# A hybrid attention and convolution layer on one core: one tile's split moved ahead of another step, and a store issued two steps earlier

## The chip, the cores and the metric

The kernel runs on one core of one Trainium2 chip. The metric is the time of one execution on the device in microseconds (us). The engines are TensorE (PE, matrix products, with its weight loads as PEld), VectorE (DVE), ScalarE (ACT), GpSimd (POOL) and SyncE (SP, which here only issues DMAs). ACT issues DMAs too, between its own operations and in the same order of instructions.

## The reference

One layer over 4096 tokens of width 1024, in float32:

```python
h = rmsnorm(x, norm_w)
proj = h @ w_in                      # u, g_b, g_c, z_conv, q, k, v, z_attn: 512 columns each
y_conv = short_gated_conv(u, g_b, g_c, conv_w, conv_b) * silu(z_conv)
q, k = rmsnorm(q per head), rmsnorm(k per head)
for window, dilation in ((128, 1), (512, 4), (2048, 16)):
    o_i, lse_i = dilated_window_attention(q, k, v, rel_bias, window, dilation)
o = sum over i of softmax(lse)_i * o_i
y = concat(y_conv, o * silu(z_attn))
out = x + y @ w_out
```

There are 8 heads of 64; each query attends to a band of keys on both sides, in blocks of 128 queries by 256 keys.

## The kernel before

Products that need more than half precision are made of two float16 parts, `hi` and `lo`, so that each product is three matmuls (hi·hi, hi·lo, lo·hi).

**Phase A** (up to about 690 us of the trace) goes over 32 tiles of 128 tokens (loop at L594). For a tile `t` it makes, on PE, four groups of 24 matmuls (`mm`, lines 410 to 412): q, k, v and z. Each group accumulates in one of eight PSUM banks. Tiles 0 and 1 are done ahead of the loop, side by side. The tile's input is its normalised `x`, transposed: `x_split(t)` copies `x` times its norm to float16 on ACT (L391, tile `xs`), takes the difference on DVE (L392), and issues two DMA transposes on SP (L394) that write the tile `hb`, which the matmuls of tile `t` read. Inside the loop, `x_split(t + 2)` stands at the end of tile `t`, so tile 4 is split in the loop's first turn, tile 2 in front of the loop, and tile 3 in the first turn (`t == 2`) by a line of its own, next to `late()`.

`late()` holds what is left to do for tiles 0 and 1: `v_sums` (eight matmuls of L484 into bank 3, read by DVE at L485), `v_scales` (L488, L489), `post_v` of tiles 0 and 1 (L457 to L461, with a store to `v_d`), `v_gate` (L493, L494), and `post_z` of tiles 0 and 1 (L465 on ACT, L466 on DVE, L467 on POOL, then a store to `sz_d` on SP). L485 frees bank 3 for tile 2's z group; L457 of tile 0 frees bank 4 for tile 3's q group. `post_qk1` (L424, L426) starts the work on a tile's q or k behind its matmuls; `post_z` ends a tile. In some turns a task for the convolution's weights stands behind `x_split`, with one sum on DVE (L275) that a small matmul on PE (L278) reads.

**Phase B** (about 690 to 1840 us) goes over 384 units `u` of attention (loop at L1162), 8 units to a group, 48 groups. While PE works through attention it fills its time with the matmuls of the convolution (`fill`, lines 854 to 856). In step `u` stand, in this order: `p_hi(u)` on ACT (L1098, or L1092 for each third unit), `p_lo(u)` on DVE, `exps(u + 1)` on ACT (L1066), a DMA transpose of the probabilities on SP (`tr`, L1112, tile `pt`; each third unit goes through PE instead, `tr_pe`, L1086, which reads `L`, the output of L1066), `av(u - 3)` on PE (L1123 to L1125) with its eviction on ACT (L1126) into `ot`, the products of `u + 2` (L1044, L1045) and its `logits` on DVE (L1057), which write into `ot` too. `ot` has two buffers, one per group; a group's outputs go to memory by `o_store` (L1137, L1139 or L1141, on ACT's queue), and the next group but one can only write the buffer when the store has read it. `b` is a unit's place in its group; since `av` runs three units late (`LAG = 3`), the last eviction of a group is in step `b == 2` of the next group. In step `b == 3`, `load_v` issues the loads of the next group's `vt`, three to eight DMAs on ACT's queue.

Every DMA of the program, on whichever queue, is given one of eight completion semaphores in turn (`DMAHW0` to `DMAHW7`), and one that gets a semaphore again waits on its issuing engine until the DMA eight places before it has landed. The order of the work is written by hand; each engine runs its instructions in that order.

Of the kernel before, what the change touches and what calls it, by code (L numbers as in the profile page):

```python
# [56 lines left out]
LAG = 3  # L57
# [8 lines left out]
def tile_hybrid_block(  # L66
# [135 lines left out]
    def load_x(t):  # L202
        XT[t] = xts[t % 3]
        nc.sync.dma_start(XT[t], xf[t * 128:(t + 1) * 128, :])
# [149 lines left out]
    def stats1(t):  # L354
        sq = pa.tile([128, D], F16, name="xsq")
        ss = pa.tile([128, 1], F32, name="ssx", bufs=2)
        nc.scalar.activation(sq, XT[t], AF.Square, accum_out=ss)
        RX[t] = rsqrt1(ss, 1, 1.0 / D, "x")
# [4 lines left out]
    def h_views(t):  # L363
        c = t // 2
        b = (hb[c] if t % 2 else h_room(c, c % 3))[:, t % 2]
        HT[t] = (b[:, 0], b[:, 1])
        return HT[t]
# [20 lines left out]
    def x_split(t):  # L388
        parts = [pa.tile([128, D], F16, name=f"xs{i}", bufs=2) for i in range(2)]
        r = RX.pop(t)  # L390
        nc.scalar.activation(parts[0], XT[t], AF.Copy, scale=r)  # L391
        nc.vector.scalar_tensor_tensor(parts[1], XT[t], r, parts[0], op0=OP.mult, op1=OP.subtract)  # L392
        for to, src in zip(h_views(t), parts):
            nc.sync.dma_start(to, src, transpose=True)  # L394
# [5 lines left out]
    def h_store(c):  # L400
        nc.sync.dma_start(hT_d[c], hb.pop(c).rearrange("p a b k n -> p (a b k n)"))
# [20 lines left out]
    def post_qk1(t, which, p):  # L422
        sq = pa.tile([128, 512], F32, name="wk", bufs=3)
        nc.scalar.activation(sq, p, AF.Square)  # L424
        ss = pa.tile([128, H], F32, name="ssq", bufs=2)
        nc.vector.tensor_reduce(ss, sq.rearrange("p (h d) -> p h d", h=H), axis=AX.X, op=OP.add)  # L426
        PQ[t, which] = (p, rsqrt1(ss, H, rqs[:, int(which == "k"), 0:1], "q"))

    def post_qk2(t, which):
        p, rs = PQ.pop((t, which))  # L430
        c = rqs[:, int(which == "k")]
        r = rsqrt2(rs, c[:, 1:2], c[:, 2:3])
        qn = pa.tile([128, H, DH], F32, name="wk", bufs=3)
        nc.vector.tensor_tensor(qn, p.rearrange("p (h d) -> p h d", h=H),
                                r[:, :, None].to_broadcast([128, H, DH]), op=OP.mult)
        if which == "q":
            nc.vector.tensor_tensor(qn, qn, cvec[:, None, :].to_broadcast([128, H, DH]), op=OP.mult)  # L437
        w, hi, lo = (4, slice(0, 4, 3), slice(1, 3)) if which == "q" else (6, slice(0, 4, 2), slice(4, 6))
        q16 = pa.tile([128, 4, w, DH], F16, name="h16", bufs=3)
        qn = qn.rearrange("p (a b) d -> p a b d", b=2)  # L440
        nc.scalar.activation(q16[:, :, hi], qn, AF.Copy)  # L441
        nc.vector.tensor_tensor(q16[:, :, lo], qn, q16[:, :, hi], op=OP.subtract)
        if which == "k":
            nc.gpsimd.tensor_copy(q16[:, :, 1:4:2], q16[:, :, hi])
        Q16[t, which] = q16
# [8 lines left out]
    def post_v(t, p):  # L454
        v16 = pa.tile([128, H, 128], F16, name="h16", bufs=3)
        v32 = pa.tile([128, 512], F32, name="wk", bufs=3)
        nc.vector.tensor_tensor(v32, p, vs, op=OP.mult)  # L457
        pv = v32.rearrange("p (h d) -> p h d", h=H)
        nc.scalar.activation(v16[:, :, 0:DH], pv, AF.Copy)
        nc.vector.tensor_tensor(v16[:, :, DH:128], pv, v16[:, :, 0:DH], op=OP.subtract)  # L460
        nc.sync.dma_start(v_d[t * 128:(t + 1) * 128], v16)  # L461

    def post_z(t, p):
        sz = pa.tile([128, 512], F32, name="wk", bufs=3)
        nc.scalar.activation(sz, p, AF.Tanh, scale=cz[:, 1:2])  # L465
        nc.vector.scalar_tensor_tensor(sz, sz, 1.0, p, op0=OP.add, op1=OP.mult)  # L466
        nc.gpsimd.tensor_tensor(sz, sz, vinv, op=OP.mult)  # L467
        nc.sync.dma_start(sz_d[t * 128:(t + 1) * 128], sz)
# [12 lines left out]
    def v_sums():  # L481
        pcs = bank(3, [128, 512])
        for n in range(KT):
            nc.tensor.matmul(pcs, ones16, VA[n], start=n == 0, stop=n == KT - 1)  # L484
        nc.vector.tensor_scalar(vinv, pcs, 1e-30, None, op0=OP.max)  # L485

    def v_scales():
        nc.vector.reciprocal(vs, vinv)  # L488
        nc.vector.tensor_scalar(vs, vs, V_SCALE / H_SCALE, None, op0=OP.mult)  # L489

    def v_gate():

        nc.vector.tensor_scalar(vinv, vinv, inv[:, 6:7], inv[:, 7:8], op0=OP.mult, op1=OP.mult)  # L493
        nc.vector.tensor_scalar(vinv, vinv, 0.5 * H_SCALE / (V_SCALE * P_SCALE), None, op0=OP.mult)  # L494
# [7 lines left out]
    def bias_load(g):  # L502
        if g == 0:
            nc.vector.memset(rb, 1.0)
            nc.sync.dma_start(rb[0:NBK, :], rel_bias)
        OH[g] = wpool.tile([128, 512], F32, name="w31")
        nc.sync.dma_start(OH[g][0:NBK + 1, 0:VEC], onehot[:, g, :])
# [77 lines left out]
    def late():  # L585
        v_sums()
        v_scales()
        post_v(0, pv[0])
        post_v(1, pv[1])
        v_gate()  # L590
        post_z(0, pz[0])
        post_z(1, pz[1])

    for t in range(2, NT):  # L594
        b0 = 4 * (t % 2)
        post_qk1(t, "q", pq)
        if t + 3 < NT:
            load_x(t + 3)
        post_qk2(t, "q")
        pk = mm((t,), b0 + 1, 5)[0]  # L600
        if t == 2:
            late()
            x_split(3)
        if 6 <= t < 9:
            bias_load(t - 6)
        post_qk1(t, "k", pk)
        if t + 2 < NT:
            stats1(t + 2)
        if t > 3:
            run_tasks(tw, per // 2)  # L610
        pv = mm((t,), b0 + 2, 6)[0]
        qk_store(t, "q")
        if t % 2 and t + 1 < NT:
            h_store(t // 2)
        post_qk2(t, "k")
        if t + 2 < NT:
            stats2(t + 2)
        post_v(t, pv)
        pz = mm((t,), b0 + 3, 7)[0]
        post_z(t, pz)  # L620
        if t + 2 < NT:
            x_split(t + 2)
        if t > 3:
            run_tasks(tw, per - per // 2)
        if t + 1 < NT:
            pq = mm((t + 1,), 4 - b0, 4)[0]
        qk_store(t, "k")
        if 6 <= t < 9:
            bias_rows(t - 6)
        if 10 <= t < 10 + H:  # L630
            bias_copies(t - 10)
        if t == 12:
            taps()
        if t == 13:
            nc.vector.tensor_scalar(cw, cw, 0.5, None, op0=OP.mult)
        if t == NT - 3:
            load_h(0)
        if t == NT - 2:
            load_h(1)
# [318 lines left out]
    for gi, (pr, g, grp) in enumerate(groups):  # L958
        d = DILS[g]
        for b in range(8):  # L960
# [8 lines left out]
            U = dict(pr=pr, g=g, d=d, grp=grp, gi=gi, b=b, vidx=vidx, kn=256, c0=0)  # L969
# [192 lines left out]
    for u in range(NU):  # L1162
        U = units[u]
        p_hi(u)
        p_lo(u)
        if u + 1 < NU:
            exps(u + 1)
        if not by_pe(u):
            tr(u)
        fill(pers[u] / 2)  # L1170
        if u >= LAG:
            av(u - LAG)
        if u + QZB + 2 < NU and units[u + QZB + 2]["d"] == 1 and units[u + QZB + 2]["b"] % 2 == 0:
            q_order(u + QZB + 2)
        if u + QZB + 1 < NU:
            q_alone(u + QZB + 1)
        if u + 6 < NU:
            k_dense(u + 6)
        if u + 2 < NU:
            qk(u + 2)  # L1180
        if u + 3 == NU:
            c_room2()
            sz_load(0)
        if u + 2 < NU:
            logits(u + 2)
        if u + 3 == NU:
            c_room4()
        if u > 8 and U["b"] == LAG + 1:
            o_store(U["gi"] - 1)
        if U["b"] == LAG and U["gi"] + 1 < len(groups):  # L1190
            VT[U["gi"] + 1] = load_v(*groups[U["gi"] + 1])
        fill(pers[u] / 2)
        if u + 1 < NU and by_pe(u + 1):
            tr_pe(u + 1)
        if state["done"]:
            for _ in range(4):
                if bg:
                    bg.pop(0)()
        pr = U["pr"]
        if u == 4:  # L1200
            load_bias(0, 0)
            load_bias(0, 1)
        for a, b, at, rate in CHUNKS:
            p, n = divmod(u - at, 96)
            for n in range(rate * n, min(5, rate * n + rate) if 0 <= p < 3 else 0):
                load_stacks(p + 1, n, a, b)
        n = u - LAG
        if n > 0 and n % 32 == 0 and n // 32 <= 9:
            load_bias((n - 32) // 96 + 1, order[0][(n // 32 - 1) % 3])
# [107 lines left out]
```

## Time and profile before

| | us |
|---|---|
| median of three runs | 2181.21 |
| the three runs | 2181.21, 2185.51, 2176.76 |
| the profiled execution | 2186.28 |
| its span, from the first to the last instruction | 2184.5 |

The mean granted clock of TensorE is 0.987 of full speed. In rows of the timeline stand: start in us, duration in us, engine, line, operation, written and read tile, count, and in square brackets how long the engine was idle before it and what ended that; an engine's name with a q behind it is its instruction queue, where its DMAs are issued. Rows of grouped waits give the total, the number and the longest. Rows of stretches give for each engine the busy time and, in brackets, the number of instructions (PE, PEld, DVE, ACT, POOL), then the granted clock, the share of the DMA engines and GB/s.

### The profile page before, as it was taken

The page shows a single profiled execution, that of the slowest core. Times are in us where ns is not written, and L with a number is a line of the kernel's source. Part 1 is how long each engine was busy: PE and PEld are TensorE (multiplying, and loading weights), DVE is VectorE, ACT ScalarE, POOL GpSimd, SP SyncE. Part 2 cuts the span into 40 slices and gives each one's busy share as a digit, 9 for nine tenths or more (in the row PEclk, how much of TensorE's full clock was granted, in tenths as well). Part 3 has the DMA queues.
Part 4 walks back from the last instruction along what each step waited for, and adds up shares of the span by engine and source line. Part 5 has one row for each costly group of instructions (what it writes and reads, how often), then busy time and mean ns, then how long its engine had stood idle before and what let it go on. Part 6 is the DMA issues. An engine that isn't in the chain of part 4 may idle for free. (4 is left out here: it accounts for less than half of the span.)

```text
span 2184.5 us, 48540 instructions
## 1 busy us (share of the span) xinstructions
PE 2081.3 (95%) x17462; PEld 1533.7 (70%) x17462; DVE 1441.1 (66%) x4032; ACT 1069.4 (49%) x3095; POOL 851.8 (39%) x1635
## 2 busy tenths in 40 slices
PE   7699999999999989998999999999999999999999
PEld 3244444444444778888888888888888887788887
DVE  7755666656665366766677656675667676887776
ACT  6323333433432167666677656666667674222221
POOL 0322232332323265433554346433453454343332
PEclk9899999999999999999999999999999999999999
DMA  5255489975554877799877998769977687787775
GB/s 204 88 153 174 142 176 172 221 177 161 169 169 137 179 138 164 147 164 186 164 160 137 172 194 136 153 120 176 204 141 129 122 171 225 233 256 244 244 244 183
DMA packets 692397, 378.34 MB, mean 173 GB/s; under 512 B 470721, under 2 KB 636732, under 8 KB 688060
## 3 DMA queue, kind: packets, MB, share of 16 engines
q1 hardware_dynamic: 570788, 304.72, 62.0%
q10 hardware_dynamic: 121368, 70.53, 13.7%
q8 instruction: 137, 2.24, 0.4%
q14 instruction: 104, 0.85, 0.1%
HBM read 157.77 MB, written 110.39 MB: 123 GB/s over the span
## 5 line engine op out<-in xcount | busy, mean ns | idle before, releaser
L854 PE MATMUL bank<-hb,w 128*128 128x256 f16 x2048 | 560.9, 274 | 0.3 <-ACT cu L861 0.3
L856 PE MATMUL bank<-hb,w 128*128 128x256 f16 x2048 | 560.8, 274 | 0.0
L855 PE MATMUL bank<-hb,w 128*128 128x256 f16 x2048 | 560.8, 274 | 0.0
L410 PE MATMUL bank<-wa,hb 128*128 128x512 f16 x1024 | 391.4, 382 | 14.9 <-DMA hb<-xs 11.4
L1057 DVE CUSTOM_DVE_ANT_0 L<-bank,bt,alpha 128x256 f32<-128x256 f32 (+1 forms) x768 | 319.0, 453 | 126.3 <-PE bank L1045 74.1
L1066 ACT ACTIVATE L<-L,ot 128x256 f32<-128x256 f32 (+1 forms) x768 | 364.2, 476 | 60.0 <-DVE ot L1057 58.4
L412 PE MATMUL bank<-wa,hb 128*128 128x512 f16 x1024 | 391.2, 382 | 0.8 <-DMA hb<-xs 0.7
L411 PE MATMUL bank<-wa,hb 128*128 128x512 f16 x1024 | 390.9, 382 | 0.3 <-DVE wa L301 0.2
L1018 POOL COPY qz<-qk 64x128 f16<-64x128 f16 x512 | 163.9, 320 | 152.9 <-PE bank L1045 134.6
L1108 DVE SCALAR_TENSOR_TENSOR src<-L,src 128x512 f16<-128x512 f32 (+1 forms) x256 | 171.3, 669 | 71.6 <-ACT src L1098 67.5
L856 PEld LDWEIGHTS <-w 128*128 128x128 f16 x2048 | 201.2, 98 | 24.0
L855 PEld LDWEIGHTS <-w 128*128 128x128 f16 x2048 | 201.2, 98 | 22.8 <-issue 0.5
L854 PEld LDWEIGHTS <-w 128*128 128x128 f16 x2048 | 201.3, 98 | 20.7
L238 POOL TENSOR_TENSOR rs_rq<-rs_mq,mhalf 128x8 f32<-128x8 f32 x64 | 104.9, 1639 | 268.4 <-DVE rs_mq L237 261.4
L410 PEld LDWEIGHTS <-hb 128*128 128x128 f16 x1024 | 101.6, 99 | 136.4 <-DMA hb<-xs 13.8
L1123 PE MATMUL bank<-vt,pt 128*128 128x64 f16 x1536 | 176.6, 194 | 18.9 <-DMA pt<-src 16.3
L412 PEld LDWEIGHTS <-hb 128*128 128x128 f16 x1024 | 100.6, 98 | 125.3 <-issue 4.4
L411 PEld LDWEIGHTS <-hb 128*128 128x128 f16 x1024 | 100.8, 98 | 123.5 <-issue 5.5
L1125 PE MATMUL bank<-vt,pt 128*128 128x64 f16 x1536 | 176.6, 194 | 0.0
L1124 PE MATMUL bank<-vt,pt 128*128 128x64 f16 x1536 | 176.5, 194 | 0.0
L1098 ACT ACTIVATE src<-L 128x512 f16<-128x512 f32 (+1 forms) x256 | 148.4, 580 | 52.4 <-issue 25.2
L441 ACT ACTIVATE h<-wk 128x512 f16<-128x512 f32 x64 | 40.3, 630 | 257.2 <-DVE wk L437 152.3
(211 smaller groups left out, 4440.1 us busy)
## 6 DMA issues: line engine op xcount, KB each, us to landing
o_d<-ot ACTq DMA_DIRECT2D x32, 528.0 KB, 6.1
qk<-o_d SPq DMA_DIRECT2D x63, 264.0 KB, 4.4
hT<-hb SPq DMA_DIRECT2D x16, 1024.0 KB, 4.1
wst<-in_w_in_dram SPq DMA_DIRECT2D x64, 256.0 KB, 3.2
hb<-hT SPq DMA_DIRECT2D x16, 1024.0 KB, 6.4
qk<-in_x_dram SPq DMA_DIRECT2D x32, 512.0 KB, 5.5
qk_d<-h SPq DMA_DIRECT2D x128, 96.0 KB, 2.1
vt<-v_d ACTq DMA_DIRECT2D x48, 256.0 KB, 5.8
```

The source lines that it names most:

```text
L410: nc.tensor.matmul(p, hi[:, kt, :], w[:, 0], start=kt == 0, stop=False)
L411: nc.tensor.matmul(p, hi[:, kt, :], w[:, 1], start=False, stop=False)
L412: nc.tensor.matmul(p, lo[:, kt, :], w[:, 0], start=False, stop=kt == KT - 1)
L854: nc.tensor.matmul(pt, w_h, hi[:, :, kt], start=kt == 0, stop=False)
L855: nc.tensor.matmul(pt, w_h, lo[:, :, kt], start=False, stop=False)
L856: nc.tensor.matmul(pt, w_l, hi[:, :, kt], start=False, stop=kt == KT - 1)
L1057: nc.vector.tensor_tensor_reduce(out=L[:, i], in0=p[i][:, 0:kn], in1=bias[:, U["b0"]:U["b0"] + kn], scale=alpha, scalar=BIG, op0=OP.add, o ...
L1066: nc.scalar.activation(L[:, i], L[:, i], AF.Exp, scale=-1.0, bias=ot[:, b, i, DH:DH + 1], accum_out=ot[:, b, i, DH + 1:DH + 2])
L1108: nc.vector.scalar_tensor_tensor(src[:, 1, :, c], ST.pop(u), P_SCALE, src[:, 0, :, c], op0=OP.mult, op1=OP.subtract)
L1123: nc.tensor.matmul(p[:, i], hi, v[:, 0:DH], start=j == 0, stop=False)
L1124: nc.tensor.matmul(p[:, i], hi, v[:, DH:], start=False, stop=False)
L1125: nc.tensor.matmul(p[:, i], lo, v[:, 0:DH], start=False, stop=j == 1)
```

## The change

Two edits. In the loop's first turn `x_split(3)` now stands ahead of `late()`; and `o_store` of the previous group moves from step `b == LAG + 1` (4) to step `b == LAG - 1` (2), the step in which that group's last eviction stands.

```diff
         if t == 2:
+            x_split(3)
             late()
-            x_split(3)
...
-        if u > 8 and U["b"] == LAG + 1:
+        if u > 8 and U["b"] == LAG - 1:
             o_store(U["gi"] - 1)
         if U["b"] == LAG and U["gi"] + 1 < len(groups):
             VT[U["gi"] + 1] = load_v(*groups[U["gi"] + 1])
```

On SP, in the first turn of phase A's loop, the two transposes into `hb` move past the stores of tiles 0 and 1 (`v_d` and `sz_d`); the numbers in the names count the tiles made:

```order
 L204 DMA hb_144<-in_x_dram 128x1024
-L461 DMA v_d<-h_886 128x1024
+L394 DMA_TRANSPOSE hb_646<-xs_874 128x8x128
+L394 DMA_TRANSPOSE hb_646<-xs_875 128x8x128
 L461 DMA v_d<-h_892 128x1024
+L461 DMA v_d<-h_898 128x1024
 L468 DMA sz_d<-wk 128x512 x2
-L394 DMA_TRANSPOSE hb_646<-xs_910 128x8x128
-L394 DMA_TRANSPOSE hb_646<-xs_911 128x8x128
 L452 DMA qk_d<-h_846 128x1x256 x4
```

They stood behind four stores and now stand ahead of them, right behind the load of a tile of `x`.

On DVE, at the same place, the split's difference (L392) moves ahead of the whole of `late()`:

```order
 L442 TENSOR_TENSOR h_846<-wk,h_846 128x4x128
-L485 TENSOR_SCALAR vinv<-bank_874 128x512
+L392 SCALAR_TENSOR_TENSOR xs_875<-xt,rs_rx,xs_874 128x1024
+L485 TENSOR_SCALAR vinv<-bank_880 128x512
 L488 RECIPROCAL vs<-vinv 128x512
 L489 TENSOR_SCALAR vs<-vs 128x512
 L457 TENSOR_TENSOR wk<-bank_524,vs 128x512
```

L485, L488, L489 and the first L457 now stand behind it; on ACT, L391 moves in the same way ahead of the first L459.

On ACT, in phase B, around steps `b == 2` to `b == 4` of the fourth group, before (with the semaphores that each waits for):

```order
L1126 ACTIVATE ot<-bank_8437 128x2x64 [waits PE_49]
L824 DMA y_d<-cc 128x256 [waits DMAHW0_49,Pool_49]
L1098 ACTIVATE src_6574<-L 128x2x192 [waits DMAHW5_49,Activation_49]
L1066 ACTIVATE L,ot<-L,ot 128x192 [waits DVE_49] x2
L1126 ACTIVATE ot<-bank_8491 128x2x64 [waits PE_49]
...
L949 DMA vt<-v_d 32x8x256 [waits DMAHW0_49]
L952 DMA vt<-v_d 32x256 [waits DMAHW1_49]
...
L1126 ACTIVATE ot<-bank_8546 128x2x64 [waits PE_49]
L1137 DMA o_d_84<-ot 512x1x132 [waits DMAHW2_49]
L1137 DMA o_d_84<-ot 512x1x132 [waits DMAHW3_49,Activation_49]
```

And of the change at the same place:

```order
L1126 ACTIVATE ot<-bank_8437 128x2x64 [waits PE_49]
L1137 DMA o_d_84<-ot 512x1x132 [waits DMAHW0_49,Activation_49]
L1137 DMA o_d_84<-ot 512x1x132 [waits DMAHW1_49,Activation_49]
L824 DMA y_d<-cc 128x256 [waits DMAHW2_49,Pool_49]
L1098 ACTIVATE src_6574<-L 128x2x192 [waits DMAHW5_49]
L1066 ACTIVATE L,ot<-L,ot 128x192 [waits DVE_49] x2
L1126 ACTIVATE ot<-bank_8493 128x2x64 [waits PE_49]
...
L949 DMA vt<-v_d 32x8x256 [waits DMAHW0_49]
L952 DMA vt<-v_d 32x256 [waits DMAHW1_49]
```

The two stores move from behind the load of `vt` to ahead of it, right behind the eviction on which they wait (`Activation`). They take the semaphores 0 and 1, for which the load's fifth and sixth DMA then wait; before, the stores took the semaphores 2 and 3 of the load's first two DMAs. Over the program, 13 stores waited so for a load one step old, and in the change 14 DMAs of loads wait so for a store one step old.

## The prediction

> **What bounds the kernel now.** I read the page's table of engines first, then the waits of TensorE (PE), then the stretches of the run, then the timeline around two places.
>
> ```profile
> PE 2081.3 (95%) x17462; PEld 1533.7 (70%) x17462; DVE 1441.1 (66%) x4032; ACT 1069.4 (49%) x3095; POOL 851.8 (39%) x1635
> PE bank L1086 <- ACT L L1066: 22.9, 28, 3.8
> PE bank L1123 <- DMA pt<-src: 16.3, 18, 2.9
> PE bank L410 <- DMA hb<-xs: 11.4, 1, 11.4
> DVE L L1057 <- DMA o_d<-ot: 38.7, 20, 5.1
> 200.00:700.00 500.00, 496.00 (x2291) 224.03 (x2290) 313.81 (x710) 179.98 (x328) 149.06 (x122) 1.00 0.70 172
> ```
>
> PE is busy for 95% of the span, and for 496 of the 500 us between 200 and 700, so an edit can only pay by shortening a pause of PE. (A row of waits gives the sum, the number and the longest.) The longest single pause, 11.4 us, is PE waiting at L410 for `hb`, the transposed copy that `x_split` makes. The largest wait near the other edit, 38.7 us for the stores of `ot`, is VectorE's (DVE), not PE's: it pays only where PE is late because of it. The profiled execution took 2186.28 us (span 2184.5), 5.1 us above the median of the three runs, 2181.21; a measurement of this kernel can tell about 0.5%, 10.9 us, from no change.
>
> **First edit: the fourth tile's split ahead of the late work.** The timeline of PE, then of SP, ACT, DVE and POOL, around the pause:
>
> ```profile
> 92.67 0.38 PE L410 MATMUL bank<-wa,hb 128*128 128x512 f16 x1
> 97.63 0.38 PE L412 MATMUL bank<-wa,hb 128*128 128x512 f16 x1
> 109.36 0.61 PE L410 MATMUL bank<-wa,hb 128*128 128x512 f16 x1 [11.35 <-DMA hb<-xs]
> 114.74 0.42 PE L410 MATMUL bank<-wa,hb 128*128 128x512 f16 x1
> 103.28 2.52 SPq L468 DMA_DIRECT2D sz_d<-wk  x2
> 106.32 2.61 SPq L394 DMA_TRANSPOSE hb<-xs  x2
> 90.39 0.63 ACT L441 ACTIVATE h<-wk 128x512 f16<-128x512 f32 x1 [5.24 <-DVE wk L437]
> 100.72 1.14 ACT L391 ACTIVATE xs<-xt,rs_rx 128x1024 f16<-128x1024 f32 x1
> 62.85 1.28 DVE L392 SCALAR_TENSOR_TENSOR xs<-hb,rs_rx,xs 128x1024 f16<-128x1024 f32 x1 [1.22 <-ACT xs L391]
> 91.66 0.68 DVE L485 TENSOR_SCALAR vinv<-bank 128x512 f32<-128x512 f32 x1
> 96.23 0.69 DVE L457 TENSOR_TENSOR wk<-bank,vs 128x512 f32<-128x512 f32 x1
> 102.42 1.91 DVE L392 SCALAR_TENSOR_TENSOR xs<-xt,rs_rx,xs 128x1024 f16<-128x1024 f32 x1
> 101.99 3.47 POOL L467 TENSOR_TENSOR wk<-wk,vinv 128x512 f32<-128x512 f32 x2 [14.02 <-DVE wk L466]
> ```
>
> Before, ACT's copy (100.72) comes behind the late evictions, DVE's difference at 102.42, and the two transposes stand on SP behind the two `sz_d` stores, which wait for POOL's 3.47 us. They go out at 106.32, and PE starts at 109.36, 3.0 us behind.
>
> After, step by step. ACT: L391 follows L441, which ends at 91.02, so it runs to 92.1. DVE: L392 starts there; POOL is idle then, as at 62.85, so I take 1.28 us (to 93.4), not the 1.91 with POOL at work. SP: the first transpose goes out at about 92.3 and lands by 95.3, the second 1.3 us later. So `hb` is there before PE wants it. What is late next is L485: it frees the bank of the next group (tile 2's z, first matmul 92.67; L485 ends at 92.34). It moves from 91.66 to about 93.4, +1.7, so that group starts at about 94.2 and its 24 matmuls last to 99.4. The q group of tile 3 then also needs L457 (96.23, +1.7, done at 98.6) for its bank, so it starts at 99.4 instead of 109.36: **10.0 us**. Behind the old pause twelve matmuls ran at half pace (109.36 to 114.74, 0.45 us each with a short wait, against (97.63 − 92.67)/23 = 0.216): 5.38 − 12 × 0.216 = **2.8 us** more. PE is 12.8 us ahead at the end of that group.
>
> The new pause of some 1.5 us ahead of tile 2's z could slow PE itself:
>
> ```profile
> 65.82 0.38 PE L410 MATMUL bank<-wa,hb 128*128 128x512 f16 x1 [1.49 <-DVE wk L434]
> 67.08 0.61 PE L412 MATMUL bank<-wa,hb 128*128 128x512 f16 x1 [0.68 <-DMA hb<-xs]
> 70.05 0.59 PE L410 MATMUL bank<-wa,hb 128*128 128x512 f16 x1
> ```
>
> Here pauses of 1.49 and 0.68 us were followed by eight matmuls at (70.05 − 67.08)/7 = 0.42 us: (0.42 − 0.216) × 8 = 1.7 us lost. I take no loss and keep 1.7 for the range. The Trainium skill (TensorE: Matmul & The Clock Gate, Part 1: The HAM clock gate) has the clock halve after an idle window of about 3.4 us; by that rule the pause of 1.5 us costs nothing and PE's 12.8 stands, by the rows above it is 11.1.
>
> Does the lead last? DVE, not PE, sets the next places:
>
> ```profile
> 114.22 2.15 DVE L392 SCALAR_TENSOR_TENSOR xs<-hb,rs_rx,xs 128x1024 f16<-128x1024 f32 x1 [0.33 <-ACT xs L391]
> 118.27 0.69 DVE L426 TENSOR_REDUCE ssq<-wk 128x8 f32<-128x512 f32 x1 [1.89 <-ACT wk L424]
> 133.90 0.69 DVE L466 SCALAR_TENSOR_TENSOR wk<-wk,bank 128x512 f32<-128x512 f32 x1 [0.47 <-ACT wk L465]
> 138.99 0.69 DVE L426 TENSOR_REDUCE ssq<-wk 128x8 f32<-128x512 f32 x1 [1.92 <-ACT wk L424]
> 220.60 0.15 DVE L275 TENSOR_REDUCE wtot<-wss 128x1 f32<-128x8 f32 x1
> 220.80 0.58 PE L278 MATMUL bank<-wtot,ones 128*128 128x1 f32 x2 [4.00 <-DVE wtot L275]
> ```
>
> POOL's L467 moves by up to +1.7 with L466, and with it what DVE does for tile 2's k and v: the split of tile 4 (114.22) comes at about 115.8, ends at 118.0, and its second transpose lands near 121.5, while PE (99.4 + 4 × 24 × 0.216 = 120.1) wants it with the third matmul, at 120.5: up to 1.0 us of a new pause. At 220.80 PE already waits 4.0 us for DVE's L275, so from there on **the gain is what DVE gains**, not PE. DVE's chain of tile 3 starts at 118.0 instead of 118.27 (0.3 us). Beyond that it gains the pauses in which it waited for PE's results: 1.9 us ahead of a tile's q (tiles 4 to 7) and 0.5 ahead of its z (tiles 3 to 7), that is 4 × 1.9 + 5 × 0.5 = 10.1. So L275 comes 10.4 us earlier (11.3 if POOL, with DVE quieter, delays tile 2 by 0.8 less). PE, 11.8 ahead, waits about 5.4 instead of 4.0 us there. **First edit: 10.5 us**, between 8 (all losses at once) and 11.5. From 200 us on PE is again the bound, so the lead is carried to the end.
>
> **Second edit: the stores two steps earlier.**
>
> ```profile
> 799.04 0.59 ACTq L1137 DMA_DIRECT2D o_d<-ot  x1
> 1817.32 0.38 ACTq L1141 DMA_DIRECT2D o_d<-ot  x1
> o_d<-ot ACTq DMA_DIRECT2D x32, 528.0 KB, 6.1
> 1252.06 8.20 SPq L1112 DMA_TRANSPOSE pt<-src  x2
> 1260.97 0.42 DVE L1057 CUSTOM_DVE_ANT_0 L<-bank,bt,alpha 128x192 f32<-128x192 f32 x1 [5.15 <-DMA o_d<-ot]
> 1261.91 0.23 PE L1123 MATMUL bank<-vt,pt 128*128 128x64 f16 x1 [2.88 <-DMA pt<-src]
> 1258.00:1260.00 2.00, 1.02 (x10) 0.67 (x7) 0.00 (x0) 0.31 (x1) 0.00 (x0) 1.00 1.42 174
> ```
>
> The 47 groups' stores inside the loop are issued from 799.04 to 1817.32, 22.1 us apart, so a step is 2.8 us and the store goes out 5.5 us earlier, and ahead of the next group's load of `vt` on ACT's queue rather than behind it. The longest of DVE's waits for a store is 5.15 us, so all 20 should go, 38.7 us of DVE. What is it worth to PE? At the longest one PE was itself waiting, 2.88 us, but for a transpose that was in the DMA engines together with load and store (the two at 1252.06 took 8.20 us to issue, and the window's DMA share, the last number but one, is 1.42): the same bytes stay. Behind most of the 20 waits PE shows no pause, so I count DVE's 38.7 at nothing. What can pay is ACT: a store issued behind the load holds ACT while it should run the exponentials for the next transpose on PE:
>
> ```profile
> 846.62 0.88 PE L1086 MATMUL bank<-identf,L 128*128 128x128 f32 x4 [1.04 <-ACT L L1066]
> 1642.61 0.33 PE L1086 MATMUL bank<-identf,L 128*128 128x128 f32 x1 [0.70 <-ACT L L1066]
> ```
>
> Of the 28 waits of L1086 for L1066, eleven (the first and the last are shown) begin 2 to 5 us behind a store's issue, 7.1 us in all. The load's issues lie ahead of them too, so I give the store half: **3.5 us**.
>
> Against it: the store now waits for the eviction just ahead of it on ACT, so ACT's next operations stand behind some 0.3 us and the issue (0.38 to 1.2 us), in a step where ACT is otherwise idle before its next eviction; and in the built program 14 of the load's DMAs now share a completion semaphore with a store one step old and wait for it (13 stores waited so for a load before; the change takes that away). Bounds: nothing of the 7.1 and five more us in waits that are new (−5), or all 7.1 and the third of the 16.3 us for `pt` that a shorter backlog could spare (+12).
>
> Sum: 10.5 + 3.5 = 14 us; 2186.3 − 14 = 2172.3 for an execution like the profiled one, 2181.2 − 14 = **2167 us** for the median.
>
> **Rivals.**
> *The burst only moves.* Load and store stay 2.8 us apart, the transposes for `pt` queue as long at another step, ACT's wait for its eviction eats the 3.5: gain 10.5, 2171. For it: share 1.42 above. The Trainium skill (DMA: Bandwidth & Descriptors, Queues, rings and completion order) says that the rows of SP and ACT share the same 16 engines in turn, packet by packet; by that rule an earlier store buys no bandwidth and the sum would be 2171; the 8.20 us agree.
> *The lead is half lost before 220.* The half pace at 94 us (1.7), the new pause at tile 4 (1.0), and slower chains of DVE: 7 us of the first edit, none of the second: 2174.
> *Transposes gain too.* A store done before the load starts shortens the backlog later in the group; half of the 16.3 us of waits for `pt` goes: 14 + 8 = 22, 2159.
> *Slower: ACT is held by the store.* If a store lands 6.1 us behind its issue as before, the 14 loads that share its semaphore (2.8 us behind) stand 3.3 us each, 46 us of ACT; if half reaches PE through L1086, +23 − 10.5: 2194. It decides once a store takes longer than the load needs to reach its fifth DMA, some 5 us. Against it: the 6.1 was measured behind a load.
>
> **How the numbers follow.** Forecast 0.45, burst only moves 0.25, half lost 0.17, transposes gain 0.08, slower 0.05. The forecast and the transposes are faster by over 0.5%; the second case lies at the bound and is split; the third is within. So 0.65 faster, 0.30 same, 0.05 slower. The range follows from the bounds: 8 − 5 = 3 us of gain at the least, 11.5 + 12 = 23.5 at the most, so 2178 to 2157; only the slower case lies outside.
>
> **What would show it.** Right: the pause of 11.35 us at L410 gone, tile 3's q at about 99.4, a pause of 1 to 2 us ahead of L410 near 94, L278 about 10 us earlier with a pause of 5 instead of 4; no row of DVE waiting for `o_d<-ot`; the 22.9 us of L1086 at 17 to 21. Wrong: tile 3's q later than 102; L278's pause at 8 or more (then DVE kept its old times); rows of ACT standing ahead of L949 or L952, with L1086's total above 25; or the `pt` waits far from 16.

## The result, and the profile after

| | before | after |
|---|---|---|
| median of three runs, us | 2181.21 | 2205.24 |
| the three runs, us | 2176.76 to 2185.51 | 2202.80 to 2212.60 |
| ratio, 95% interval | | 1.0118 [1.0095, 1.0142] |
| span of the profiled execution, us | 2184.5 | 2201.0 |

The change made the kernel 24 us slower; the prediction was 14 us faster, with a range that ended at 2178.

**The first edit came out.** The timeline of PE in the kernel after, at the two places that the prediction named (start, duration, engine, line, operation; in square brackets the pause ahead and what ended it):

```profile
94.18 0.38 PE L412 MATMUL bank<-wa,hb 128*128 128x512 f16 x1
95.16 0.38 PE L410 MATMUL bank<-wa,hb 128*128 128x512 f16 x1 [0.60 <-DVE vinv L485]
209.48 0.59 PE L278 MATMUL bank<-wtot,ones 128*128 128x1 f32 x2 [4.39 <-DVE wtot L275]
```

And the stretch in which PE had stood still, in a row of the windows (stretch and its length, then busy time of PE, PEld, DVE, ACT and POOL, then PE's granted clock, the share of the DMA engines and GB/s), first of the kernel after, then of the kernel before:

```profile
99.00:110.00 11.00, 11.00 (x52) 5.00 (x51) 6.61 (x16) 3.94 (x7) 4.62 (x4) 1.00 0.30 110
```

```profile
99.00:110.00 11.00, 0.64 (x2) 0.13 (x2) 7.70 (x15) 4.97 (x8) 5.98 (x5) 0.60 0.47 144
```

PE works through all 11 us of it, and L278 comes at 209.48 instead of 220.80, **11.3 us earlier**. So what was lost, 16.5 us of span and those 11.3, some 28 us, was lost later.

**The second edit lost it.** The page's row of engines and the rows of grouped waits (total, times, longest) of the kernel after:

```profile
PE 2084.9 (95%) x17462; PEld 1534.8 (70%) x17462; DVE 1445.6 (66%) x4032; ACT 1069.2 (49%) x3095; POOL 849.9 (39%) x1635
PE bank L1086 <- ACT L L1066: 32.6, 28, 5.5
PE bank L1123 <- DMA pt<-src: 20.9, 23, 2.8
PE bank L1123 <- ACT ot L1126: 8.3, 5, 3.1
ACT pt L1092 <- DMA vt<-v_d: 29.8, 5, 7.7
```

DVE's waits for `o_d<-ot`, 38.7 us before, are gone without a row left, as intended. But PE now waits 32.6 us at L1086 for ACT's exponentials (22.9 before) and 8.3 us at L1123 for ACT's evictions (0.9 before). ACT itself stands 29.8 us ahead of L1092, the longest 7.7, with the load of `vt` as what ended it. One such place, on the timelines of ACT, SP and PE in the kernel after:

```profile
983.15 0.38 ACTq L1139 DMA_DIRECT2D o_d<-ot  x1
985.14 0.63 ACTq L939 DMA_DIRECT2D vt<-v_d  x1
985.82 1.18 ACTq L940 DMA_DIRECT2D vt<-v_d  x1
987.03 4.02 ACTq L942 DMA_DIRECT2D vt<-v_d  x1
991.10 0.61 ACTq L943 DMA_DIRECT2D vt<-v_d  x1
991.75 0.47 ACT L861 ACTIVATE cu<-bank,inv 128x256 f32<-128x256 f32 x1 [6.12 <-issue]
...
985.82 3.98 SPq L1112 DMA_TRANSPOSE pt<-src  x1
989.85 3.76 SPq L661 DMA_TRANSPOSE qk<-qk_d  x1
...
993.29 0.93 PE L1086 MATMUL bank<-identf,L 128*128 128x128 f32 x4 [4.02 <-ACT L L1066]
```

And the same load in the kernel before, with the store behind it:

```profile
987.32 0.64 ACTq L939 DMA_DIRECT2D vt<-v_d  x1
987.99 0.95 ACTq L940 DMA_DIRECT2D vt<-v_d  x1
988.98 0.72 ACTq L942 DMA_DIRECT2D vt<-v_d  x1
989.74 0.66 ACTq L943 DMA_DIRECT2D vt<-v_d  x1
992.40 0.38 ACTq L1139 DMA_DIRECT2D o_d<-ot  x1
```

Read the first block from the top. The store goes out, and the load follows 2.0 us later, while the store's bytes are moving. The third DMA of the load takes 4.02 us to issue instead of 0.72, at the moment when SP's two transposes take 3.98 and 3.76 us. The load lasts from 985.14 to 991.71, 6.6 us instead of 3.1. ACT does nothing else for 6.12 us, and PE stands 4.02 us for an exponential that is queued behind. In other groups it is not one long issue but a stand (time in which ACT's queue waits) between two issues: the load at 1233.42 issues three DMAs, then nothing for 3.44 us.

Over the 48 loads, from ACT's timeline (from the first issue of a load to the end of its last): 139.2 us before, 178.3 after. Of the 39 us more, 15.0 are longer issues (128.1 to 143.1, each DMA by itself) and 24.1 are stands between issues (11.1 to 35.2). The stands of over 0.15 us can be put down to the completion that the DMA behind each waits for: after, 23.0 us (18 stands) a transpose into `pt`, 5.2 us (3) a transpose of L661, 1.5 us (3) a store, 0.3 us (1) a `y_d`; before, 5.5 us (7), all for `pt`. All queues take turns at the same eight semaphores, so ACT stands for DMAs of SP whose data the load does not need.

### The profile page after: what moved, and what is told of

Its sections match the earlier page's. It is cut to its first block, busy times and chain, and to the rows that moved or that the text cites. A ratio compares the mean times of both kernels' runs of the same rounds, so it can differ in the third digit from the quotient of the medians.

```text
span 2201.0 us, 48575 instructions
## 1 busy us (share of the span) xinstructions
PE 2084.9 (95%) x17462; PEld 1534.8 (70%) x17462; DVE 1445.6 (66%) x4032; ACT 1069.2 (49%) x3095; POOL 849.9 (39%) x1635
## 5 line engine op out<-in xcount | busy, mean ns | idle before, releaser
L410 PE MATMUL bank<-wa,hb 128*128 128x512 f16 x1024 | 389.9, 381 | 4.3 <-ACT wa L300 2.1
L1066 ACT ACTIVATE L<-L,ot 128x256 f32<-128x256 f32 (+1 forms) x768 | 363.7, 476 | 34.3 <-DVE ot L1057 32.7
L1123 PE MATMUL bank<-vt,pt 128*128 128x64 f16 x1536 | 176.9, 194 | 32.1 <-DMA pt<-src 20.9
L410 PEld LDWEIGHTS <-hb 128*128 128x128 f16 x1024 | 101.4, 99 | 124.7 <-issue 4.1
L412 PEld LDWEIGHTS <-hb 128*128 128x128 f16 x1024 | 100.5, 98 | 124.4 <-issue 3.5
L411 PEld LDWEIGHTS <-hb 128*128 128x128 f16 x1024 | 100.5, 98 | 123.6 <-issue 5.2
L1104 DVE SCALAR_TENSOR_TENSOR pt<-bank,pt 128x512 f16<-128x512 f32 x128 | 88.4, 691 | 132.9 <-ACT pt L1092 132.6
```

The source lines that it names most:

```text
L410: nc.tensor.matmul(p, hi[:, kt, :], w[:, 0], start=kt == 0, stop=False)
L411: nc.tensor.matmul(p, hi[:, kt, :], w[:, 1], start=False, stop=False)
L412: nc.tensor.matmul(p, lo[:, kt, :], w[:, 0], start=False, stop=kt == KT - 1)
L1066: nc.scalar.activation(L[:, i], L[:, i], AF.Exp, scale=-1.0, bias=ot[:, b, i, DH:DH + 1], accum_out=ot[:, b, i, DH + 1:DH + 2])
L1123: nc.tensor.matmul(p[:, i], hi, v[:, 0:DH], start=j == 0, stop=False)
```

## Experiments

Three theories stood at first. **A**: the load's DMAs hold ACT longer when they are issued while the store is in flight. **B**: ACT is held by the store itself, which waits for the eviction just ahead of it. **C**: the store's bytes make the `pt` transposes late by themselves. All kernels differ from the kernel after unless the diff says otherwise; each ratio is to the kernel before on the same chip, with its 95% interval. The runs were made on four chips, on which the kernel before took 2181.8 to 2188.1 us, so a difference of a few us between two runs' times is read from the ratios.

**1. The first edit alone.**

```diff
-        if u > 8 and U["b"] == LAG - 1:
+        if u > 8 and U["b"] == LAG + 1:
             o_store(U["gi"] - 1)
```

> Only the first edit: the fourth tile's split ahead of the late work, the store back in step 4. All theories: the pause of 11.4 us at L410 is gone, L278 near 209.5 instead of 220.8, and the time is 2181 - 11 = 2170 us (ratio 0.995). If instead it is 2181 or more, the first edit has a cost that the first 225 us do not show.

Measured 2172.55 us, ratio 0.9952 [0.9934, 0.9971]; L278 at 209.75; loads 142.6 us; L1086 for L1066 24.5 us. The first edit gives what was forecast for it, 0.0048 × 2181 = 10.5 us (6 to 14 by the interval). This kernel is the yardstick for what follows.

**2. The second edit alone.**

```diff
         if t == 2:
-            x_split(3)
             late()
+            x_split(3)
```

> Only the second edit: the store in step 2, the split where it was. All theories: about 11 us above the whole change, 2205 + 11 = 2216 us (ratio 1.016); waits of L1086 for L1066 near 33 us and of L1123 near 32, as in the whole change.

Measured 2224.41 us, ratio 1.0181 [1.0160, 1.0202]; loads 182.4 us, L1086 35.5 us. The second edit by itself costs 39 us (2224.41 − 2185.02 of the kernel before on that chip), and in both kernels that have it the loads take longer than in the same kernel without it, by 43 us here (139.2 to 182.4) and by 36 us in the change (142.6 to 178.3).

**3. Both edits, the load two steps later.**

```diff
-        if U["b"] == LAG and U["gi"] + 1 < len(groups):
+        if U["b"] == LAG + 2 and U["gi"] + 1 < len(groups):
             VT[U["gi"] + 1] = load_v(*groups[U["gi"] + 1])
```

> Both edits, and the load of vt in step 5 instead of 3, so the store has three steps (8 us) to land before the load is issued. Theory A (the load's DMAs hold ACT longer because they are issued while the store is in flight): the load's issues take back their 39 us (178 to 140 us over the 48 loads) and the time is 2165 to 2175 us. Rival B (ACT is held by the store's wait for the eviction just ahead of it): nothing changes, 2200 to 2210. Rival C (the store's bytes slow the transposes for pt by themselves): L1123's waits for pt stay at 20 us or more and the time at 2190 to 2205.

Measured 2176.77 us, ratio 0.9953 [0.9932, 0.9974], a little above A's range; loads 139.1 us, waits for `pt` 19.6 us. The store stands where the change has it, right behind its eviction, and the loss is gone, down to the ratio of the yardstick: B and C fall, since both leave the load out.

**4. Both edits, the store in the load's step, directly ahead of it.**

```diff
-        if u > 8 and U["b"] == LAG - 1:
+        if u > 8 and U["b"] == LAG:
             o_store(U["gi"] - 1)
```

> Both edits, but the store in step 3, directly ahead of the load; the eviction on which it waits is one step old. Theory A: the load stands closer behind the store than in the change, so its issues take 180 us or more and the time is 2200 to 2225. Rival B: the store no longer waits, 2170. Rival C: about as the change, 2195 to 2210.

Measured 2260.02 us, ratio 1.0347 [1.0310, 1.0384], more than A expected; loads 197.7 us; L1086 78.1 us in 42 waits. On ACT's timeline:

```profile
1256.56 0.38 ACTq L1139 DMA_DIRECT2D o_d<-ot  x1
1256.97 0.62 ACTq L939 DMA_DIRECT2D vt<-v_d  x1
1257.64 1.88 ACTq L940 DMA_DIRECT2D vt<-v_d  x1
1259.56 1.73 ACTq L942 DMA_DIRECT2D vt<-v_d  x1
1261.33 0.78 ACTq L943 DMA_DIRECT2D vt<-v_d  x1
1262.16 0.60 ACT L1092 ACTIVATE pt<-bank 128x512 f16<-128x512 f32 x1 [5.39 <-PE bank L1044]
```

Here nothing stands between issues; the issues themselves are long. Over all loads they take 176.9 of the 197.7 us. The bracket names PE, which had long been done; what ended the 5.39 us is the last issue, at 1262.11.

**5. The store directly behind the load.**

```diff
-        if u > 8 and U["b"] == LAG - 1:
-            o_store(U["gi"] - 1)
         if U["b"] == LAG and U["gi"] + 1 < len(groups):
             VT[U["gi"] + 1] = load_v(*groups[U["gi"] + 1])
+        if u > 8 and U["b"] == LAG:
+            o_store(U["gi"] - 1)
```

> Both edits, but the store goes in the third step of the group, directly behind the load of vt instead of one step ahead of it. What is tested: whether it is the order (store ahead of the load) or the nearness of the two that holds ACT. Theory A (a load whose issues come while a store is in flight holds ACT): nothing is in flight ahead of the load, so its issues take 139 to 145 us in all as in the kernel before and with the first edit alone, the waits of L1086 for L1066 stay at 23 to 28 us, time about 2172 (2165 to 2178), ratio 0.993 to 0.998. Rival D (load and store must not be near each other, in whatever order): the store's issue now stands behind the load's bytes, ACT is held by the store instead of the load, L1086's wait goes over 35, time 2190 to 2215, ratio 1.004 to 1.016.

Measured 2207.21 us, ratio 1.0119 [1.0084, 1.0155]: D's number, not A's. The loads take 142.6 us as in the yardstick, so A's statement about them holds, and yet the kernel is as slow as the change, with 50.5 us at L1086. ACT's timeline shows why:

```profile
1232.47 0.62 ACTq L939 DMA_DIRECT2D vt<-v_d  x1
1233.12 0.66 ACTq L940 DMA_DIRECT2D vt<-v_d  x1
1233.83 0.69 ACTq L942 DMA_DIRECT2D vt<-v_d  x1
1234.55 0.61 ACTq L943 DMA_DIRECT2D vt<-v_d  x1
1235.26 0.57 ACTq L1139 DMA_DIRECT2D o_d<-ot  x1
1235.87 0.60 ACT L1092 ACTIVATE pt<-bank 128x512 f16<-128x512 f32 x1 [3.13 <-PE bank L1045]
```

No issue is long here, but five in a row take 3.4 us, more than a step of 2.8. So A is too narrow: what counts is how long ACT is held in one piece, whatever makes the piece long (theory **H**, for hold).

**6. The store in two halves.**

```diff
-        if u > 8 and U["b"] == LAG - 1:
-            o_store(U["gi"] - 1)
+        if u > 8 and U["b"] == LAG - 1:
+            o_store(U["gi"] - 1, 4)
+        if U["b"] == LAG + 3:
+            o_store(U["gi"], 0)
...
-            nc.scalar.dma_start(dap(o_d[g], grp * R + base, [[4 * R, 128], [512 * R, 8], [1, RW]]), src)
+            nc.scalar.dma_start(dap(o_d[g], grp * R + base + lo * 512 * R, [[4 * R, 128], [512 * R, 4], [1, RW]]), src[:, lo:lo + 4, :])
```

> Both edits, but a group's store is cut in two: the first four units' outputs go out in step 6 of their own group, the last four in step 2 of the next one, where the change has the whole store. So about half the bytes are in flight when the load is issued in step 3. Theory A with a cost by the bytes in flight: the load's issues take about 159 us in all (half way from 140 to 178), the time lies half way between 2173 and 2205: 2188 (2181 to 2195), ratio 1.000 to 1.006. Theory A with a point from which it counts (half a store has left the engines one step later): loads 140 to 148, time 2170 to 2178. If it is the number of DMAs in flight and not their bytes: loads 175 or more, time 2200 to 2215.

Measured 2168.68 us, ratio 0.9939 [0.9916, 0.9962], a little under all three expectations; loads 153.9 us, between two of them. (The stores of the other two kinds of groups and the last store are halved likewise.) L1086 is back at 24.9 us, and the waits for `pt` fall to 12.3 us (18.8 in the yardstick). With half the bytes ahead of the load the loss is gone altogether. This does not show what the load pays for each byte: the loads are still some 11 us longer than in the yardstick, and the shorter waits for `pt` hide it.

**7. The store issued by SP.**

```diff
-            nc.scalar.dma_start(dap(o_d[g], grp * R + base, [[4 * R, 128], [512 * R, 8], [1, RW]]), src)
+            nc.sync.dma_start(dap(o_d[g], grp * R + base, [[4 * R, 128], [512 * R, 8], [1, RW]]), src)
```

> Both edits with the store in step 2, but issued by SP instead of ACT. Theory A1 (ACT's own DMA queue stands behind its own store, so a load issued from the same queue is held): loads back at 139 to 148 us, L1086 for L1066 at 23 to 28, time 2168 to 2180, ratio 0.993 to 0.999. Theory A2 (the store's bytes fill the 16 DMA engines that all queues share, and the completion semaphores that loads and transposes share come back late): loads stay at 165 us or more, time 2195 to 2210, ratio 1.006 to 1.013. If SP's transposes are held by the store in front of them, the waits of L1123 for pt go over 35 us.

(The stores of the other two kinds of groups likewise.) Measured 2204.85 us, ratio 1.0110 [1.0082, 1.0138], the change's time; loads 170.3 us. A1 falls: the load is held behind the store from whichever queue the store came. The Trainium skill (DMA: Bandwidth & Descriptors, Issuing engines are not separate DMA queues) says that DMAs of all issuing engines run on the same 16 DMA engines; this run agrees, 2204.85 beside 2205.24.

**8. The load spread over four steps.**

```diff
-        if U["b"] == LAG and U["gi"] + 1 < len(groups):
-            VT[U["gi"] + 1] = load_v(*groups[U["gi"] + 1])
+        if U["b"] == LAG + 1 and U["gi"] + 1 < len(groups):
+            VT[U["gi"] + 1] = load_v(*groups[U["gi"] + 1], 4)
+        if U["b"] > LAG and LQ:
+            for a in LQ.pop(0):
+                nc.scalar.dma_start(*a)
```

(`load_v` puts its DMAs into the list `LQ` in four parts instead of issuing them.)

> Both edits with the store in step 2, and the load of vt spread: its 3 to 8 DMAs go out in steps 4, 5, 6 and 7 (one or two in each) instead of together in step 3. Theory A (ACT held in one piece by a load is what PE pays for): no step holds ACT for more than some 1.5 us, the waits of L1086 for L1066 go under 20 us (24.5 with the first edit alone), time 2160 to 2170, ratio 0.990 to 0.995. Rival (the same ACT time is only spread, and each piece hits another exponential): L1086 at 25 to 32, time 2172 to 2180.

Measured **2132.12 us**, ratio 0.9779 [0.9748, 0.9811], far under both expectations. PE's waits (the lines stand ten further down in this kernel):

```profile
PE bank L1133 <- DMA pt<-src: 13.3, 11, 3.3
PE bank L1096 <- ACT L L1076: 4.5, 4, 3.2
```

and ACT's timeline in one load:

```profile
1199.23 0.61 ACTq L1204 DMA_DIRECT2D vt<-v_d  x1
1199.27 0.19 ACT L1076 ACTIVATION_READ_ACCUMULATOR L<-L,ot 128x1 f32 x1
1199.37 0.26 ACT L1136 ACTIVATE ot<-bank 128x128 f32<-128x128 f32 x1
1199.94 0.63 ACT L1108 ACTIVATE src<-L 128x512 f16<-128x512 f32 x1 [0.31 <-ACT ot L1136]
...
1201.98 0.62 ACTq L1204 DMA_DIRECT2D vt<-v_d  x1
1202.70 0.63 ACT L1108 ACTIVATE src<-L 128x512 f16<-128x512 f32 x1 [0.45 <-ACT ot L1136]
```

ACT stands idle 0.31 and 0.45 us at the two issues shown. The load's issues still take 100.5 us of ACT in all, but in pieces. The wait for exponentials, 24.5 us in the yardstick and 22.9 in the kernel before, was nearly all the load's: 4.5 us are left. In one piece the load cost the yardstick some 40 us (2172.55 − 2132.12), as much as the second edit added. It is the spreading and not the later step that pays, since run 3 has the load in step 5, in one piece, at 2176.77.

**9. The same, with the store where it was before (step 4).** The edit is against the kernel of 8.

```diff
-        if u > 8 and U["b"] == LAG - 1:
+        if u > 8 and U["b"] == LAG + 1:
             o_store(U["gi"] - 1)
```

> The first edit and the load spread over steps 4 to 7, with the store where it was before (step 4). What is tested: what the second edit is worth once the load is not in one piece behind it. Over the kernels so far with the first edit, the time follows what stretches of back-to-back DMA issues on ACT last beyond 2 us each, summed: 1.9 us at 2132 (spread load), 40.4 at 2172.6 (first edit alone), 65.6 at 2205 (the change), 129.7 at 2260 (store directly ahead of the load), so about 1 us of time for 1 us of it. Theory H (ACT held in one piece is what costs): the store with one or two load DMAs behind it lasts some 1.5 to 2.5 us, excess under 10 us, DVE's waits for o_d return (about 40 us) and cost PE little; time 2130 to 2142, ratio 0.977 to 0.982. Rival S (the store's early place is worth something once it hits no load): time 2145 to 2160, ratio 0.983 to 0.990, DVE's L1057 waits for o_d standing right ahead of waits of PE.

Measured 2140.45 us, ratio 0.9782 [0.9764, 0.9800], the same ratio as with the early store within the intervals (the times, 8 us apart, are from two chips): without a load in one piece beside it, the store's place is worth nothing that can be measured. DVE's waits for `o_d` came back with 8.2 us only, not 40.

**10. Spread load and half stores** (the edits of 6 and 8 together).

> Both edits, the load spread over steps 4 to 7, and the store cut in two as in the run with half stores (first four units in step 6, the rest in step 2). Theory H: nothing of ACT is left in one piece over 2 us in the kernel with the spread load, so halves bring nothing; 16 or more additional DMAs cost some ACT time: 2130 to 2140, ratio 0.977 to 0.982. Rival A2 (bytes in flight delay SP's transposes for pt also with a spread load; L1123 waits 13.3 us for pt there): those waits fall under 8 us and the time to 2120 to 2129, ratio 0.972 to 0.976.

Measured **2123.20 us**, ratio 0.9705 [0.9691, 0.9719], the fastest of all: the time and the `pt` waits of A2, not H's. (H had expected nothing from the halves.) The waits:

```profile
PE bank L1096 <- ACT L L1076: 7.2, 10, 2.7
PE bank L1133 <- DMA pt<-src: 5.7, 6, 3.2
```

The wait for exponentials did not fall (7.2 us, 4.5 in run 8), so H has nothing left to give here; what the halves save is `pt`, 13.3 to 5.7 us. Bytes in one burst do have a price of their own, beside the hold.

**11. The load issued by SP, otherwise the change.**

```diff
-            nc.scalar.dma_start(vt[up, 0:8, :], v_rows(pr, grp, [[4 * VR, 64], [512 * VR, 8], [1, 256]]))
+            nc.sync.dma_start(vt[up, 0:8, :], v_rows(pr, grp, [[4 * VR, 64], [512 * VR, 8], [1, 256]]))
```

(All DMAs of the load likewise.)

> The change with its load of vt in step 3 as it stands, but issued by SP's queue instead of ACT's: the same bytes at the same step behind the same store, and ACT free of them. Theory H (it is ACT being held that PE pays for): the waits of L1086 for L1066 fall under 10 us (32.6 with the change, 4.5 with the spread load). SP is held instead, by some 145 to 180 us in 48 pieces, with the transposes for pt behind them: L1123's waits for pt go from 20.9 to between 30 and 60 us; time 2140 to 2185, ratio 0.981 to 1.002. Rival A3 (the bytes of load and store together delay everything, whoever issues them): L1086 stays over 25 us, time 2195 or more, ratio 1.006 or more.

Measured 2151.71 us, ratio 0.9828 [0.9808, 0.9848]:

```profile
PE bank L1123 <- DMA pt<-src: 28.4, 23, 3.3
PE bank L1086 <- ACT L L1066: 6.6, 4, 3.2
```

The same bytes go out at the same step of the program behind the same store, and 53 us are gone with ACT free of them, although SP's transposes come later (28.4 us, 20.9 in the change). On the chip the load starts a little later behind the store, at the median 4.1 us instead of 2.3; run 3, with 7.7 us, shows that the distance alone does not do it, since L1086 waits 29.8 us there. The same section of the Trainium skill has it that another issuing engine saves only the time that issuing takes, usually small beside the DMA. Here it is not small: in the change the issues of one load take 3.0 us (143.1 over 48 loads), beside a median of 5.3 from a DMA's issue to its landing, and where the two differ the measurement decides.

**12. ACT held, with no DMA.** The kernel of 8, and in step 3 seven copies of a scratch tile that nothing reads:

```diff
+        if U["b"] == LAG and U["gi"] + 1 < len(groups):
+            for _ in range(7):
+                nc.scalar.activation(hold, hold, AF.Copy)
```

> The kernel with both edits and the spread load (2132 us), with seven copies of a scratch tile of 128 x 256 in place on ACT added in step 3, where the change has its load: some 2.8 to 3.4 us of ACT in one piece, 47 times, with no byte more in the DMA engines. Nothing reads the scratch tile. Theory H (ACT held in one piece costs, by what it lasts beyond 2 us, about 1 us per us): excess 47 x (0.8 to 1.4) = 38 to 66 us, the waits of L1086 for L1066 back over 20 us (4.5 with the spread load), time 2160 to 2198, ratio 0.990 to 1.006. Rival A2 (the bytes of load and store side by side are what costs, and ACT has room for 3 us): L1086 under 10 us, time 2130 to 2142, ratio 0.976 to 0.982.

Measured 2174.65 us, ratio 0.9968 [0.9952, 0.9984]. On ACT's timeline and in PE's waits:

```profile
1205.48 3.09 ACT L1204 ACTIVATE hold<-hold 128x256 f16<-128x256 f16 x7
```

```profile
PE bank L1098 <- ACT L L1078: 29.9, 35, 2.5
```

Some 3.1 us of ACT in one piece, 47 times, 51.7 us beyond 2 us each, cost 42.5 us (2174.65 − 2132.12) and bring the wait for exponentials back from 4.5 to 29.9 us. No byte was added: holding ACT is enough. (The same copies spread over several steps were not run; that ACT's work in pieces costs little is shown by run 8, for issues.)

**All kernels together.** "Hold beyond 2 us" is worked out from ACT's timeline between 690 and 1900 us: every stretch of DMA issues with no other row of ACT starting between them, from the start of the first to the end of the last, less 2 us where it is longer, summed. (2 us is a choice, the idle part that ACT has in a step of 2.8.)

| kernel | hold beyond 2 us | exponentials late for PE | `pt` late for PE | median us |
|---|---|---|---|---|
| 8, load spread | 1.9 | 4.5 | 13.3 | 2132.1 |
| 11, load on SP | 1.3 | 6.6 | 28.4 | 2151.7 |
| 9, load spread, store in step 4 | 5.1 | 5.2 | 19.1 | 2140.5 |
| 10, load spread, half stores | 8.8 | 7.2 | 5.7 | 2123.2 |
| 3, load in step 5 | 37.5 | 29.8 | 19.6 | 2176.8 |
| 1, first edit alone | 40.4 | 24.5 | 18.8 | 2172.6 |
| 6, half stores | 47.8 | 24.9 | 12.3 | 2168.7 |
| 12, copies (1.9 and 51.7) | 53.6 | 29.9 | 16.3 | 2174.7 |
| the change | 65.6 | 32.6 | 20.9 | 2205.2 |
| 7, store on SP | 65.6 | 34.2 | 25.7 | 2204.9 |
| 5, store behind the load | 78.3 | 50.5 | 8.2 | 2207.2 |
| 4, store ahead in the load's step | 129.7 | 78.1 | 5.2 | 2260.0 |

All these have the first edit (without it the kernel before has a hold of 38.4, the second edit alone one of 70.1). From first to last, 128 us more hold are 128 us more time (124 by the ratios). Where two kernels with like holds differ by much, the waits for `pt` go the same way (10 and 11); smaller differences they do not explain (the change and 7).

## Why the prediction was wrong

**First edit: right.** Pause at L410 gone, L278 11.3 us earlier (10.4 was forecast, and 11.3 for a quieter POOL), worth 10.5 us by run 1 (10.5). DVE's pauses ahead of L426 and L466 went, as forecast. That the gain reached 11.3 was not POOL: tile 2's share was late as forecast (the split of tile 4 at 115.87, 115.8 forecast), and the pauses were each worth a little more than was counted. Some details were off without weight. The new pause ahead of tile 2's z was 0.60 us instead of 1.5, since PE was itself later there (that group starts at 95.16, not 94.2, and tile 3's q 24 × 0.216 us later, at 100.3 instead of 99.4), so the question of a half pace behind it did not come up. The pause at L278 was 4.39 instead of 5.4, and the one of up to 1.0 us at tile 4 did not come. The 1.7 us that were kept for a half pace came from two pauses at 65.82 and 67.08; in the kernel after, the same two pauses (1.49 us ahead of 66.95 and 0.67 ahead of 68.21) were followed by matmuls 0.216 us apart at a granted clock of 1.00, so pauses of this size do not always bring it.

**Second edit: the step that failed is "a store issued behind the load holds ACT while it should run the exponentials ... so I give the store half: 3.5 us".** The pauses of L1086 that begin 2 to 5 us behind a store were put down to the store. But what stood on ACT ahead of them was the store's issue, 0.7 us in the mean of a group (33.0 / 48), and one step earlier the load's, of 2.9 us (139.2 / 48). The sentence "the load's issues lie ahead of them too" saw the load and still gave it only half. The runs give the load nearly all: with the load spread or on another queue, those 22.9 us fall to between 4.5 and 6.6, wherever the store stands (runs 8, 9, 11). The stores' own issues took 33.0 us before and 33.6 after: the move freed nothing there.

The sign turned on the same step. With the store taken for what holds ACT, what it does to the load when it stands ahead was priced at no more than "five more us in waits that are new". But it lengthens the load's hold, by 36 us over the 48 loads (142.6 to 178.3). The forecast of 17 to 21 us for L1086 became 32.6, with ACT standing ahead of L949 and L952 as the prediction had named for being wrong, and 3.5 us of gain became a loss of 33 (2205.24 − 2172.55; 36 by the ratios). Against run 1 the profiled span grew by 30.6 us (2201.0 − 2170.4): PE's idle time by 20.8, of which L1086 has 8.1 more, L1123 for ACT's evictions 7.4, for `pt` 2.1, for `vt` 1.3; and PE's busy time by 9.8 (2084.9 and 2075.1), with the granted clock at 0.987 instead of 0.992. Behind the pause of 4.02 us shown above, for one, the granted clock is 0.50 from 994.5 to 997.5. The prediction had no term for PE running slower behind new pauses in phase B.

**DVE's 38.7 us counted at nothing: right.** They are gone and bought nothing; run 9 has the store back in step 4 and the same time as run 8.

**The slower rival had the place, nearly the price (2194), and the wrong reason.** It let the load stand 46 us for the store's own semaphore. The load does stand, but for a store only 1.5 us; 23.0 us go to SP's `pt` transposes, which share the eight semaphores, and 15.0 us more than before to issues that are longer in themselves. What was held against it, "the 6.1 was measured behind a load", did not hold: the store lands after as before.

```profile
o_d<-ot ACTq DMA_DIRECT2D x32, 528.0 KB, 6.1
```

The median of 6.1 us is the same as in the kernel before. So the chance of 0.05 rested on one untested sentence. The lower bound of −5 us had no row behind it in which a load is issued behind a store in flight: in the trace of before no load is issued less than 15 us behind a store, so nothing there could give that bound. "The burst only moves" got its `pt` waits roughly right (16.3 to 20.9) and missed that a burst that moves can meet ACT's queue. Its 8.20 us were one row of two transposes, 3.13 and 4.10 us to issue with 1.0 us between, and so say less than it took from them. Two sums are loosely rounded, without weight: 10.4 + 0.8 is 11.2, and 2181.2 − 23.5 is 2157.7.

**What stays open.** Why an issue takes 4.02 us instead of 0.72 was not isolated. Run 7 shows that the loads are held without a store of ACT's own queue ahead of them, and the rows above show SP's issues long at the same moments. The Trainium skill (Perfetto Trace Analysis, DMA Instruction — HWDGE (DVE, Sync)) says that a reported issue includes the wait for a descriptor generator that the issuing sequencers share; the two long issues side by side fit that, but no run here separates it from DMA engines full of the store's bytes. Stands that come from the shared semaphores were not tried by themselves either, since the order of the semaphores can't be chosen from the kernel's text.

## What to carry to other kernels

Here a DMA issued from ACT held ACT like an instruction of its own. Where an engine that also computes issues DMAs, ask first how long it is held in one piece by each burst of issues, and compare that with the engine's slack in a step. A load of 3 to 8 issues in one step cost some 37 us (run 1 and run 9, ratios 0.9952 and 0.9782, which differ in the spreading alone), three and a half times what the better of the two edits brought. Before a transfer is moved, look at what is issued behind it while it is in flight, on any queue (a load 2.3 us behind the store was held here, one 7.7 us behind was not), and do not take a wait for the fault of the last row ahead of it when a longer one stands just before.

## What the runs showed of the hardware beyond what was expected

- The kernel loses about 0.8 us for each us that ACT is held beyond 2 us in a step of 2.8 (run 12: 42.5 for 51.7), although ACT is busy for only 49% of the span. By the table of all kernels, with DMA issues as the hold, it is nearer to 1 us.
- The load's issues, 0.62 us in the mean and 2.08 at the longest before, grew to 4.02 at the longest behind a store of 528 KB in flight, and to 177 us in all instead of 128 when the store stood directly ahead.
- Moving the store's issue to SP changed nothing (2204.85 and 2205.24); moving the load's issue to SP saved 53 us (2205.24 and 2151.71).
- Halving the stores brought 9 us with the spread load by the times (2132.12 and 2123.20) and 16 by the ratios (0.9779 and 0.9705, of 2181), with 7.6 us less waiting for `pt`.
